# Group factors by a selection matmul, weights kept as stored pairs, the embedding product inside the gate's tile, norm chains put off, in the tail of a hybrid encoder layer

## The chip, the cores and the metric

The kernel runs on one core of one Trainium2 chip. The metric is the device time of one execution in microseconds (us); a lower one is better. Three runs of the kernel before took 1746.35, 1748.64 and 1754.81 us, so its median is 1748.64 us.

## The reference

One layer on x of 2048 tokens by 1024 features, all in float32:

```
h = RMSNorm(x);  cB, cC, ch, cz, q, k, v, az = split(h @ W_in)      # 8 x 512 columns
yc = cB * dwconv3_causal(cC * ch)                  # gated short convolution
ya = stick_breaking_attention(q, k, v)             # 8 heads x 64
y  = group_rmsnorm(concat(yc, ya), 64) * silu(concat(cz, az))       # 16 groups a token
x1 = x + y @ W_out
gate = sigmoid(RMSNorm(x1) @ W_pg + b)
x2 = x1 + gate * (p @ W_pe)                        # p: 256 features a token
out = RMSNorm(x2)
```

Stick-breaking attention takes, for a query t and keys s < t, the weight sigmoid(z_s) times the product of (1 - sigmoid(z)) over the keys between s and t. That running product is what the kernel computes as a scan along the keys.

## The kernel before, in words

**Layout.** Features lie on the 128 partitions, tokens along the free axis. The tokens are four chunks of 512, numbered 3, 2, 1, 0 in the order in which they are worked. A matrix product of full float32 quality is made of three passes: each operand is split into a rounded high part and a low part (`wh`, `wl` for a weight tile, `hh`, `hl` for an activation), and `product` (L230) issues high by high, high by low and low by high (L234, L235, L236), each 128 by 128 against 128 by 512. A tile of 128 output features takes 8 steps of contraction, so 24 matmuls.

**Weights.** `fetch_w` (L208) loads a raw half tile of weights (128 by 512, 256 KB) from DRAM, and `split_w` (L220) makes the pair of it: ScalarE copies the high part (L225), GpSimd subtracts for the low part (L226). That is done anew for each chunk in the tail: 16 tiles (8 of W_out, numbers 32 to 39, and 8 of W_pg, numbers 40 to 47) of two halves for each of four chunks, so 128 splits.

**Order of the program.** First come the projections of chunks 3 and 2 (`workE`), then those of chunks 1 and 0 (`workL`). Then the tail: for each chunk an `out_stage` (L630, product with W_out and x1) and a `gate_stage` (L685, product with W_pg, sigmoid, the embedding product with W_pe, x2). Every stage is a generator that yields after each step of contraction. `run` (L769) pulls 0.72 or 0.92 steps of the attention generator (L534) at each yield, so attention of all heads lies between the products, up to the end of chunk 1's `out_stage`; chunk 1's `gate_stage` must wait for chunk 0's attention, and from there on there is none. `later(n, f)` calls `f` n yields afterwards. Which order each engine's queue gets in the end is decided by a scheduler that keeps dependencies; each engine works its queue in order.

**Beside the stages.** `y_prep(c)` (L570) makes the W_out operand of chunk c: it multiplies y by the group factors and by the gate, and splits it. The factors lie with tokens on partitions (`rg`), so `expand` (L585) lets GpSimd copy each factor 64 or 16 times along the free axis, and four transposes (L604) bring that to features on partitions, five times a chunk, in the one PSUM bank `aux`. The norm of x1 is a chain: squares on ScalarE (L627), added up on GpSimd (L628), `norm_r` (L152: four matmuls by ones, L156, then a power on GpSimd, L161) and `norm_spread` (L166: four transposes, L171, and a copy). The factor `rB` of it is wanted first by the evacuation of the gate's first tile (L696). The norm of x2 is the same chain, started by `final` (L740).

**The embedding product.** In `gate_stage` each tile begins with six matmuls into a bank of its own (L722 to L724) with weights that `pe_weights` (L670) loads and splits for each chunk and tile (L679, L680). That bank is one of the two `mm` banks, which the gate's own tile (`pp`) also takes.

PSUM banks before: `z` 2, `mm` 2, `tr` 2 (attention's transposes), `av` 1, `aux` 1.

## Time and profile before

| | us |
|---|---|
| median of three runs | 1748.64 |
| the profiled execution | 1747.67 |
| its span, first to last instruction | 1745.9 |
| PE busy | 1614.3 (92%) |
| DVE busy | 1217.3 (70%) |
| POOL busy | 966.2 (55%) |
| ACT busy | 855.6 (49%) |
| mean DMA traffic | 141 GB/s |

PE is TensorE, DVE is VectorE, ACT is ScalarE, POOL is GpSimd, SP is the engine that issues most transfers. The busy share of PE is an average: it is 100% in some stretches and lower in the tail, and matmuls at a lower granted clock also count as busy. So the tail's stretches, their granted clock and what ended PE's idle time there are what to read.

### The profile page before, as it was taken

What the parts mean: (1) busy time and instruction counts of PE and PEld (TensorE: products, weight loads), DVE (VectorE), ACT (ScalarE), POOL (GpSimd) and SP (SyncE); (2) the same over time, 40 slices, a digit from 0 to 9 for tenths busy, and PEclk for the clock granted to TensorE, in tenths of its full rate; (3) what the DMA queues carried; (4) which work ended last, traced back from release to release, by engine and by line L of the source; (5) the groups of instructions that cost most, each with busy time, mean ns of one, the idle gap of its engine ahead of it and who ended that gap; (6) DMA issues with size and microseconds to landing.
All of it is one profiled execution on the core that took longest, in us unless ns stands there. A gap on an engine that the chain in (4) does not pass through costs nothing. (4 is left out here: it accounts for less than half of the span.)

```text
span 1745.9 us, 23060 instructions
## 1 busy us (share of the span) xinstructions
PE 1614.3 (92%) x7634; PEld 1309.7 (75%) x7634; DVE 1217.3 (70%) x1544; ACT 855.6 (49%) x1680; POOL 966.2 (55%) x891
## 2 busy tenths in 40 slices
...
GB/s 187 147 84 175 127 163 149 111 139 166 70 138 158 145 142 142 158 146 143 82 75 92 92 85 133 176 144 158 129 227 158 162 144 191 152 146 153 240 155 73
DMA packets 138632, 246.94 MB, mean 141 GB/s; under 512 B 16656, under 2 KB 20752, under 8 KB 138512
## 3 DMA queue, kind: packets, MB, share of 16 engines
...
HBM read 180.38 MB, written 65.01 MB: 141 GB/s over the span
## 5 line engine op out<-in xcount | busy, mean ns | idle before, releaser
L234 PE MATMUL pp<-hh,wh 128*128 128x512 f32 x1008 | 421.6, 418 | 2.1 <-ACT hh L138 2.1
L235 PE MATMUL pp<-hl,wh 128*128 128x512 f32 x1008 | 402.1, 399 | 1.2 <-DVE hl L141 1.2
L236 PE MATMUL pp<-hh,wl 128*128 128x512 f32 x1008 | 401.8, 399 | 0.0
L481 DVE TENSOR_TENSOR_SCAN T<-s,carry,small 128x513 f32<-128x513 f32 x192 | 293.5, 1529 | 98.0 <-ACT s L462 94.2
L462 ACT ACTIVATE s<-z 128x512 f32<-128x512 f32 (+1 forms) x320 | 171.5, 536 | 248.8 <-PE z L460 237.6
L487 POOL TENSOR_TENSOR b<-b,T 128x512 f32<-128x512 f32 (+2 forms) x160 | 179.7, 1123 | 150.2 <-DVE T L481 110.5
L226 POOL TENSOR_TENSOR wl<-wr,wh 128x512 fp32r<-128x512 f32 x126 | 176.3, 1401 | 101.3 <-ACT wh L225 95.3
L512 DVE TENSOR_TENSOR al<-tp,ah 128x512 fp32r<-128x512 f32 (+1 forms) x320 | 188.8, 597 | 59.2 <-ACT ah L509 58.1
L236 PEld LDWEIGHTS pp<-hh,wl 128*128 128x128 f32 x1008 | 192.1, 191 | 42.6
L234 PEld LDWEIGHTS pp<-hh,wh 128*128 128x128 f32 x1008 | 192.7, 191 | 32.9 <-ACT hh L138 2.4
L235 PEld LDWEIGHTS pp<-hl,wh 128*128 128x128 f32 x1008 | 193.3, 192 | 31.5 <-DVE hl L141 3.1
L509 ACT CAST ah<-tp 128x512 fp32r<-128x512 f32 (+1 forms) x320 | 166.1, 525 | 101.5 <-PE tp L504 99.9
L485 POOL COPY carry<-T 128x1 f32<-128x1 f32 x192 | 53.4, 278 | 277.6 <-DVE T L481 236.6
L504 PE MATMUL tp<-first,b 128*128 128x128 f32 x1088 | 177.0, 277 | 28.4 <-DVE al L512 25.0
L504 PEld LDWEIGHTS tp<-first,b 128*128 128x128 f32 x1088 | 138.8, 144 | 74.0 <-DVE al L512 33.2
L464 ACT ACTIVATE b<-z 128x512 f32<-128x512 f32 (+1 forms) x320 | 169.7, 530 | 0.0
L487 DVE TENSOR_TENSOR b<-b,T 128x512 f32<-128x512 f32 (+1 forms) x160 | 149.1, 932 | 10.4 <-DVE T L481 0.5
L479 DVE TENSOR_TENSOR_SCAN T<-s,first 128x129 f32<-128x129 f32 x128 | 84.0, 658 | 61.8 <-ACT s L462 58.1
L459 PE MATMUL z<-kk,q 128*128 128x512 f32 (+1 forms) x320 | 118.7, 371 | 5.9 <-DMA kk<-qk_d 3.9
L518 PE MATMUL av<-al,vv 128*128 128x512 f32 (+1 forms) x320 | 120.1, 376 | 1.8 <-DVE al L512 1.8
L517 PE MATMUL av<-ah,vv 128*128 128x512 f32 (+1 forms) x320 | 119.3, 373 | 0.0
L460 PE MATMUL z<-kk,q 128*128 128x512 f32 (+1 forms) x320 | 119.1, 372 | 0.0
...
## 6 DMA issues: line engine op xcount, KB each, us to landing
wr<-in_wst_dram SPq DMA_DIRECT2D x128, 256.0 KB, 2.7
vv<-v_d SPq DMA_DIRECT2D x80, 256.0 KB, 3.0
kk<-qk_d SPq DMA_DIRECT2D x80, 256.0 KB, 4.0
q<-qk_d SPq DMA_DIRECT2D x64, 256.0 KB, 3.7
...
v_d<-vo SPq DMA_DIRECT2D x32, 256.0 KB, 2.4
...
yt<-y_d SPq DMA_DIRECT2D x32, 256.0 KB, 2.9
```

Source lines behind the costliest of these rows:

```text
L226: nc.gpsimd.tensor_tensor(out=wl, in0=raw, in1=wh.bitcast(F32), op=ALU.subtract)
L234: nc.tensor.matmul(pp, wh[:, sl], hh, start=(kt == 0), stop=False)
L235: nc.tensor.matmul(pp, wh[:, sl], hl, start=False, stop=False)
L236: nc.tensor.matmul(pp, wl[:, sl], hh, start=False, stop=(kt == KT - 1))
L462: nc.scalar.activation(s[:, 1:w + 1], zp[:, 0:w], AF.Sigmoid, scale=-0.125)
L464: nc.scalar.activation(bt[:, 0:w], zp[:, 0:w], AF.Sigmoid, scale=0.125)
L481: nc.vector.tensor_tensor_scan(T[:, m:w + 1], s[:, m:w + 1], zeros.to_broadcast([P, w + 1 - m]), T[:, m - 1:m] if diag else carries[h, qc] ...
L487: eng.tensor_tensor(out=bt[:, 0:w], in0=bt[:, 0:w], in1=T[:, 0:w], op=ALU.mult)
L504: nc.tensor.transpose(tp[:, j * P:(j + 1) * P], bt[:, kb * P - k0:(kb + 1) * P - k0], ident)
L509: nc.scalar.copy(ah[:, 0:nj * P], tp[:, 0:nj * P])
L512: nc.vector.tensor_tensor(out=al[:, 0:w], in0=tp[:, 0:w], in1=ah[:, 0:w].bitcast(F32), op=ALU.subtract)
L518: nc.tensor.matmul(av[:, 0:w], v[:, kb], al[:, 0:w], start=False, stop=kc == 3 and kb == 0)
```

## The change

1. **Group factors.** `y_prep` no longer lets GpSimd copy factors. VectorE splits the 16 factors of a token into high and low parts (`r2`, 32 columns), four transposes turn them to 32 partitions (`rt`), and for each of the 8 feature tiles one matmul by a constant 0/1 matrix (`sel`, 32 rows, made once at the start on GpSimd) spreads them over the features.
2. **Stored pairs.** The pairs of W_out and W_pg are made once, in chunk 3, and stored to DRAM (`store_w`). For chunks 2, 1 and 0 `split_w` loads both parts straight into the buffers that the matmuls read. The pairs of W_pe are made once, beside two of chunk 1's and 0's projections (`pe_pairs`), stored, and loaded per tile (`pe_fetch`). One raw buffer fewer, one `w1` buffer more, one key buffer fewer.
3. **Embedding product.** Its six matmuls stand after the fourth step of the gate's tile (`embed`), in a `tr` bank.
4. **Norm chains put off.** `norm_r` and `norm_spread` for x1 stand 6 and 10 yields behind the `out_stage`; the evacuation of the gate's first tile is put off by 5; `final` begins 8 yields into the next `out_stage` and takes 4 yields a tile.
5. **Banks.** `aux` is gone and `tr` has three banks, shared by attention's transposes, group factors, norms, value transposes and the embedding product.
6. **Last chunk.** Sums of squares and x2 are added on VectorE, final_g is applied by ScalarE beforehand, and the last scaling reads the spread factor from PSUM, two tiles of eight on GpSimd, with stores from two queues.
7. The last two projection tiles run side by side (`proj_two`) with chunk 3's `y_prep`, at 0.5 attention steps per yield; four rows of attention (of 320) that stood ahead of chunk 3's `out_stage` now stand behind it, and the last three rows behind the start of chunk 1's `gate_stage`, where none stood. The store of x1 goes from ScalarE's queue to SP's.

On PE, at the passage from chunk 0's `out_stage` to its `gate_stage`, before (`pp40` is the gate's first tile, `ssp4` and `rT4` are the two PE steps of the norm of x1; ahead of these rows stand the six matmuls of the embedding product):

```order
L234 MATMUL pp40_('x1', 0)_16693<-hh_('x1', 0)_0_16294,wh('x1', 0)_40_0_16602 128x512
L235 MATMUL pp40_('x1', 0)_16693<-hl_('x1', 0)_0_16295,wh('x1', 0)_40_0_16602 128x512
L236 MATMUL pp40_('x1', 0)_16693<-hh_('x1', 0)_0_16294,wl('x1', 0)_40_0_16603 128x512
L234 MATMUL pp40_('x1', 0)_16693<-hh_('x1', 0)_1_16353,wh('x1', 0)_40_0_16602 128x512
L235 MATMUL pp40_('x1', 0)_16693<-hl_('x1', 0)_1_16354,wh('x1', 0)_40_0_16602 128x512
L236 MATMUL pp40_('x1', 0)_16693<-hh_('x1', 0)_1_16353,wl('x1', 0)_40_0_16603 128x512
L156 MATMUL ssp4_16661<-small_247,acc_('x1', 0)_16297 128x2 x4
L234 MATMUL pp40_('x1', 0)_16693<-hh_('x1', 0)_2_16401,wh('x1', 0)_40_0_16602 128x512
L235 MATMUL pp40_('x1', 0)_16693<-hl_('x1', 0)_2_16402,wh('x1', 0)_40_0_16602 128x512
L171 MATMUL rT4_16671<-first_241,rr_258 128x128 x4
```

The same place after the change (`px140` and `px141` are the gate's first and second tiles, `pe0_0` the embedding product):

```order
L788 MATMUL pe0_0_16602<-ph0_0_16532,we0_0_16582 128x512
L786 MATMUL pe0_0_16602<-ph0_1_16536,we0_0_16582 128x512
L787 MATMUL pe0_0_16602<-pl0_1_16537,we0_0_16582 128x512
L788 MATMUL pe0_0_16602<-ph0_1_16536,we0_0_16582 128x512
L179 MATMUL ssp4_16615<-small_319,acc0_16216 128x2 x4
L273 MATMUL px140_0_16584<-x1hh0_4_16429,wh40_241_16558 128x512
L274 MATMUL px140_0_16584<-x1hl0_4_16430,wh40_241_16558 128x512
```

And further on, to the passage to the gate's second tile:

```order
L273 MATMUL px140_0_16584<-x1hh0_7_16575,wh40_241_16558 128x512
L274 MATMUL px140_0_16584<-x1hl0_7_16576,wh40_241_16558 128x512
L275 MATMUL px140_0_16584<-x1hh0_7_16575,wl40_241_16559 128x512
L194 MATMUL rT4_16638<-first_313,rr_331 128x128 x4
L273 MATMUL px141_0_16645<-x1hh0_0_16212,wh41_242_16585 128x512
L274 MATMUL px141_0_16645<-x1hl0_0_16213,wh41_242_16585 128x512
```

The step by ones (L156, now L179) stood behind the embedding product and two steps of the gate's tile; now it stands behind four steps and the embedding product. The transposes (L171, now L194) stood two matmuls further on; now they stand behind the whole first tile.

On SP in chunk 0's `out_stage`, before (`wr` a raw half of weights, `of` a tile of chunk 1's x2, `xr` a tile of x, `out_0` the output):

```order
L214 DMA wr('y', 0)_36_1_16368<-in_wst_dram 128x512
L133 DMA of1_6_16302<-o_d1_6_221 128x512
L759 DMA out_0_dram<-of1_3_16274 128x512
L759 DMA out_0_dram<-of1_4_16281 128x512
L759 DMA out_0_dram<-of1_5_16288 128x512
L133 DMA xr0_2_16305<-in_xt_dram 128x512
L133 DMA of1_7_16319<-o_d1_7_222 128x512
L759 DMA out_0_dram<-of1_6_16302 128x512
L133 DMA xr0_3_16361<-in_xt_dram 128x512
L214 DMA wr('y', 0)_37_0_16386<-in_wst_dram 128x512
```

And after the change (`wh` and `wl` the parts of a half tile, `wp` their place in DRAM, `x1_d` the store of x1):

```order
L256 DMA wh36_232_16335<-wp_d36_0_0_255 128x512
L256 DMA wl36_232_16336<-wp_d36_0_1_256 128x512
L708 DMA x1_d0_2_177<-xr0_2_16218 128x512
L156 DMA of1_4_16347<-o_d1_4_219 128x512
L853 DMA out_0_dram<-of1_2_16295 128x512
L256 DMA wh36_233_16356<-wp_d36_1_0_257 128x512
L256 DMA wl36_233_16357<-wp_d36_1_1_258 128x512
L156 DMA of1_5_16367<-o_d1_5_220 128x512
L853 DMA out_0_dram<-of1_3_16315 128x512
L156 DMA xr0_5_16384<-in_xt_dram 128x512
L256 DMA wh37_234_16387<-wp_d37_0_0_259 128x512
L256 DMA wl37_234_16388<-wp_d37_0_1_260 128x512
```

Each half of weights is two loads where it was one, and the stores of x1 stand in the same queue. From the first load of the W_out weights of chunk 0 to the first of its W_pg weights SP has 46 transfers before and 68 after the change (11.9 and 17.8 MB); in chunk 3's `gate_stage` 61 and 103 (15.1 and 27.0 MB). From the first load for chunk 3's `out_stage` to the end of chunk 0's, SP moves 94.7 MB before and 143.1 MB after.

The core of the diff:

```diff
-        RAWS = 3
+        RAWS = 2
...
+        def paired(t, tag):
+            return t >= OUT0 and tag[1] < 3
...
         def split_w(pool=pj, tags=("wh", "wl")):
 
-            if raws:
-                t, tag, f, raw = raws.pop(0)
-                wh, wl = [pool.tile([P, CH], F32R, tag=x, bufs=4, name=f"{x}{tag}_{t}_{f}") for x in tags]
-                nc.scalar.copy(wh, raw)
-                nc.gpsimd.tensor_tensor(out=wl, in0=raw, in1=wh.bitcast(F32), op=ALU.subtract)
-                wt[t, tag, f] = (wh, wl)
+            n = made[0]
+            if n < 2 * len(wq):
+                (t, tag), f = wq[n // 2], n % 2
+                made[0] += 1
+                wh, wl = wt[t, tag, f] = [
+                    pool.tile([P, CH], F32R, tag=x, bufs=4, name=f"{x}{t}_{n}") for x in tags]
+                if paired(t, tag):
+                    for w, d in zip((wh, wl), wp_d[t, f]):
+                        nc.sync.dma_start(w.bitcast(F32), d)
+                else:
+                    raw = raws.pop(0)
+                    nc.scalar.copy(wh, raw)
+                    nc.gpsimd.tensor_tensor(out=wl, in0=raw, in1=wh.bitcast(F32), op=ALU.subtract)
+                    if t >= OUT0:
+                        later(3, store_w, t, f, wh, wl)
             fetch_w()
+
+        def store_w(t, f, *pair):
+            for w, d in zip(pair, wp_d[t, f]):
+                nc.sync.dma_start(d, w.bitcast(F32))
...
+                    pp = bank("mm", 2, f"pp{t}_{c}")
+                    for kt in range(KT):
+                        if (i, n, kt) in ((0, 0, 0), (0, 0, 4), (1, 0, 4), (1, 1, 0)):
+                            split_w()
+                        product(pp, t, tag, c, kt)
+                        if kt == KT - 1:
+                            evacs[n](c, pp)
+                        if i:
+                            next(besides, None)
+                        yield
+            for _ in besides:
+                yield
...
                 if besides is not None:
                     next(besides, None)
                 yield
+                if kt == 3 and between is not None:
+                    yield from between()
...
+            fetch(0)
+            r2 = pj.tile([P, 4, 32], F32R, tag="r2", bufs=1, name=f"r2_{c}")
+            rs = rg[:, 4 * c:4 * c + 4]
+            nc.vector.tensor_copy(r2[:, :, 0:16], rs)
+            nc.vector.tensor_tensor(out=r2[:, :, 16:32], in0=rs, in1=r2[:, :, 0:16].bitcast(F32),
+                                    op=ALU.subtract)
+            yield
+            yield
+            turned = bank("tr", 3, f"rt{c}")
+            for b in range(4):
+                nc.tensor.transpose(turned[0:32, b * P:(b + 1) * P], r2[:, b].bitcast(F32), ident)
+            rt = buf("u", f"rs{c}", F32R, CH + 2)
+            nc.scalar.copy(rt[0:32, 0:CH], turned[0:32])
+            yield
+            yield
+            for kt in range(KT):
+                fetch(kt + 1)
+                gT = bank("tr", 3, f"gT{c}_{kt}")
+                j = max(kt - 3, 0) * P
+                nc.tensor.matmul(gT, sel[0:32, j:j + P], rt[0:32, 0:CH], start=True, stop=True)
...
+        def norm_of(slot, key):
+            assert counts[key] == KT
+            norm_r(slot, accs[key])
...
-                    squares(("x1", c), m, x1)
-                    nc.scalar.dma_start(x1_d[c][m], x1)
+                    later(1, squares, ("x1", c), m, x1, nc.vector if c == 0 else nc.gpsimd)
+                    later(2, lambda: nc.sync.dma_start(x1_d[c][m], x1))
...
-
-            def spread():
-                norm_r(slot, accs["x1", c])
-                later(3, norm_spread, slot)
-            later(2, spread)
-
-        ph, pw = {}, {}
-
-        def p_prep(c):
+            later(6, norm_of, slot, ("x1", c))
+            later(10, norm_spread, slot)
+
...
-        def pe_weights(c, m):
-            if m == KT:
-                return
-            raw = buf("w1", f"we{c}_{m}")[:, 0:2 * P]
...
-            later(3, split)
+        def pe_pairs():
+
+            for m in range(KT):
+                raw = buf("w1", f"we{m}")[:, 0:2 * P]
+                nc.sync.dma_start(raw, wpe_d[m])
+                yield
+                yield
+                t = buf("sl", f"wes{m}", F32R)
+                nc.scalar.copy(t[:, 0:2 * P], raw)
+                nc.gpsimd.tensor_tensor(out=t[:, 2 * P:4 * P], in0=raw, in1=t[:, 0:2 * P].bitcast(F32),
+                                        op=ALU.subtract)
+                yield
+                yield
+                nc.sync.dma_start(we_d[m], t.bitcast(F32))
+
+        pw = {}
+
+        def pe_fetch(c, m):
+            if m < KT:
+                pw[c, m] = buf("sg", f"we{c}_{m}", F32R)
+                nc.sync.dma_start(pw[c, m].bitcast(F32), we_d[m])
 
...
+            def embed(m):
+
+                def f():
+                    w = pw.pop((c, m))
+                    pe = bank("tr", 3, f"pe{c}_{m}")
+                    for kt in range(2):
+                        h, l = ph[c, kt]
+                        hi, lo = [w[:, (2 * i + kt) * P:(2 * i + kt + 1) * P] for i in range(2)]
+                        nc.tensor.matmul(pe, hi, h, start=(kt == 0), stop=False)
+                        nc.tensor.matmul(pe, hi, l, start=False, stop=False)
+                        nc.tensor.matmul(pe, lo, h, start=False, stop=(kt == 1))
+                        if kt == 0:
+                            yield
+                    es[m] = buf("sh", f"e{c}_{m}")
+                    nc.scalar.copy(es[m], pe)
+                    pe_fetch(c, m + 1)
+                    xs[m] = load(x1_d[c][m], f"x1r{c}_{m}")
+                    yield
+                return f
...
+            def evac(m):
+                def f(pp):
+                    later(5 if m == 0 else 0, sigmoid, m, pp)
+                return f
+
+            def sigmoid(m, pp):
+                g = buf("gg", f"g{c}_{m}")
+                nc.vector.tensor_tensor(out=g, in0=pp, in1=rB[slot], op=ALU.mult)
+                nc.scalar.activation(g, g, AF.Sigmoid, bias=b_pg[:, m:m + 1])
+                later(2, mix, m, g)
+
+            def mix(m, g):
+                x1 = xs.pop(m)
+                nc.vector.tensor_tensor(out=g, in0=g, in1=es.pop(m), op=ALU.mult)
+                o = resident[m] if c == 0 else g
+                adds.tensor_tensor(out=o, in0=x1, in1=g, op=ALU.add)
+                later(2 if c else 0, total, m, o)
+
+            def total(m, o):
+                squares(("o", c), m, o, adds)
+                if c:
+                    later(1, lambda: nc.sync.dma_start(o_d[c][m], o))
+                else:
+                    nc.scalar.activation(o, o, AF.Copy, scale=g_fin[:, m:m + 1])
+
+            pe_fetch(c, 0)
+            side = twice() if besides is not None else None
+            for m in range(KT):
+                yield from stage(GATE0 + m, ("x1", c), evac(m), side, embed(m))
+            if besides is not None:
+                for _ in besides:
+                    yield
+
...
+        def final(c):
+
+            for _ in range(8):
+                yield
+            norm_of(8 + c, ("o", c))
+            for _ in range(5):
+                yield
+            norm_spread(8 + c)
...
+                for _ in range(4):
                     yield
...
+                later(2, lambda o=o, m=m: nc.sync.dma_start(out_d[c, m], o))
+
+        def final_last():
+
+            norm_of(8, ("o", 0))
+            r = rr[:, 64:68]
+            rT = bank("tr", 3, "rT8")
+            for b in range(4):
+                nc.tensor.transpose(rT[:, b * P:(b + 1) * P], r[:, b:b + 1].to_broadcast([P, P]), ident)
+            spread = buf("rB", "rB8")
+            nc.scalar.copy(spread, rT)
+            for m in range(KT):
+                o = resident[m]
+                on_pool = m in (1, 4)
+                eng = nc.gpsimd if on_pool else nc.vector
+                eng.tensor_tensor(out=o, in0=o, in1=spread if on_pool else rT, op=ALU.mult)
+                (nc.scalar if m % 2 else nc.sync).dma_start(out_d[0, m], o)
...
@@ -800,6 +910,8 @@
                     b = besides
                     if chunks == cE and (kind, i) in (("g", 1), ("g", 2)):
                         b = (norm_later(cL[i - 1]),) * 2
+                    if chunks == cL and (kind, i) in (("g", 0), ("g", 1)):
+                        b = (pairs_e,) * 2
                     add(work, gate, t, gi, chunks, b, tiles=[(t, chunks[0])])
...
-        workL = pairs_of(cL, orderL, last=y_prep(3), first_besides=ahead(splits(0), 2))
+        pairs_e = pe_pairs()
+        workL = pairs_of(cL, orderL[:-2], first_besides=ahead(splits(0), 2))
+
+        work2 = []
+        add(work2, lambda: proj_two((3, 15), cL, (evac_b(3), evac_gate(15, 3)), ahead(y_prep(3), 2)),
+            tiles=[(3, cL[0]), (15, cL[0])])
...
             def gates(c=c):
-                p_prep(c)
-                pe_weights(c, 0)
-                tick_all()
                 return gate_stage(c, y_prep(c - 1) if c else None)
             add(tail[-1], gates, need=[(h, c - 1) for h in range(NH)] if c else [],
                 tiles=[(GATE0 + m, ("x1", c)) for m in range(KT)])
         run(workL, RATE_L)
+        run(work2, RATE_Y)
```

## Rows read from the trace of the kernel before

**Rows 1.** Busy time by stretch: us, PE, PEld, DVE, ACT, POOL, PEclk, DMA share, GB/s
```profile
950.00:1050.00 100.00, 100.00 (x493) 82.27 (x492) 86.02 (x103) 50.89 (x98) 53.70 (x53) 1.00 0.26 81
1056.50:1536.10 479.60, 417.47 (x1945) 332.76 (x1944) 385.73 (x417) 269.01 (x520) 345.44 (x307) 0.94 0.52 162
1536.10:1612.70 76.60, 65.11 (x279) 52.21 (x278) 26.43 (x34) 32.13 (x57) 52.16 (x44) 0.89 0.50 154
1612.70:1665.40 52.70, 49.42 (x212) 39.03 (x210) 25.47 (x28) 22.05 (x38) 34.10 (x26) 0.97 0.70 231
1665.40:1726.80 61.40, 58.00 (x246) 46.99 (x246) 12.90 (x16) 25.11 (x44) 44.55 (x37) 0.94 0.34 103
1726.80:1745.90 19.10, 2.98 (x12) 2.50 (x12) 6.94 (x11) 1.94 (x3) 3.54 (x3) 0.60 0.30 110
1640.00:1650.00 10.00, 9.75 (x42) 7.22 (x40) 4.48 (x6) 4.26 (x7) 5.60 (x5) 1.00 0.91 308
```
**Rows 2.** PE's waits from 1056.5 us on: waiter, releaser, us in total, times, longest
```profile
PE tp L504 <- DVE al L512: 15.3, 11, 3.0
PE pe L722 <- ACT wes L679: 12.0, 3, 7.6
PE gT L604 <- DVE yt L606: 10.1, 7, 3.7
PE ssp L156 <- POOL acc_('o', 0)_16764 L628: 5.7, 1, 5.7
PE gT L604 <- POOL rb L590: 5.6, 2, 4.8
PE ssp L156 <- POOL acc_('o', 3)_11974 L628: 5.0, 1, 5.0
PE rT L171 <- POOL rr L161: 4.9, 8, 1.4
...
PE pp_('x1', 1)_15777 L234 <- DVE g L696: 3.0, 1, 3.0
...
PE ssp L156 <- POOL acc_('x1', 1)_14862 L628: 0.8, 1, 0.8
...
PE pp_('x1', 0)_16693 L234 <- DVE xr L641: 0.3, 1, 0.3
```
**Rows 3.** PE in order of time about one stall: start, us, what, idle before
```profile
1569.63 0.79 PE L722 MATMUL pe<-ph,wes 128*128 128x512 f32 x1 [7.55 <-ACT wes L679]
...
1572.56 0.63 PE L234 MATMUL pp_('x1', 1)_15850<-hh_('x1', 1)_0_14859,wh('x1', 1)_42_0_15778 128*128 128x512 f32 x1
1572.98 0.63 PE L235 MATMUL pp_('x1', 1)_15850<-hl_('x1', 1)_0_14860,wh('x1', 1)_42_0_15778 128*128 128x512 f32 x1
...
1573.71 0.40 PE L234 MATMUL pp_('x1', 1)_15850<-hh_('x1', 1)_1_14969,wh('x1', 1)_42_0_15778 128*128 128x512 f32 x1
1573.94 0.40 PE L235 MATMUL pp_('x1', 1)_15850<-hl_('x1', 1)_1_14970,wh('x1', 1)_42_0_15778 128*128 128x512 f32 x1
```
**Rows 4.** POOL's busy time of the weights' low parts in the tail (L226)
```profile
1056.50:1726.80 670.30, 180.71 (x125) 0.94 0.51 161
```
**Rows 5.** DVE in order of time: the same operation twice
```profile
1497.35 0.75 DVE L141 SCALAR_TENSOR_TENSOR hl_('x1', 1)_3_15166<-xr,cst,hh_('x1', 1)_3_15165 128x512 fp32r<-128x512 f32 x1 [0.60 <-ACT hh_('x1', 1)_3_15165 L138]
1514.89 1.89 DVE L141 SCALAR_TENSOR_TENSOR hl_('x1', 1)_5_15351<-xr,cst,hh_('x1', 1)_5_15350 128x512 fp32r<-128x512 f32 x1 [0.20 <-ACT hh_('x1', 1)_5_15350 L138]
```
**Rows 6.** Transfers: what, count, KB each, us from issue to landing
```profile
wr<-in_wst_dram SPq DMA_DIRECT2D x128, 256.0 KB, 2.7
...
wr('y', 0)_37_0_16386<-in_wst_dram SPq DMA_DIRECT2D x1, 256.0 KB, 6.0
```
**Rows 7.** All engines in order of time, the end
```profile
1726.83 0.69 DVE L696 TENSOR_TENSOR g<-pp_('x1', 0)_17106,rB 128x512 f32<-128x512 f32 x1 [4.66 <-PE pp_('x1', 0)_17106 L236]
...
1729.08 1.26 POOL L705 TENSOR_TENSOR o<-x1r,g 128x512 f32<-128x512 f32 x1 [3.50 <-DVE g L703]
1730.38 0.63 ACT L627 ACTIVATE sq_('o', 0)_7_17139<-o 128x512 f32<-128x512 f32 x1 [2.10 <-POOL o L705]
1731.08 1.26 POOL L628 TENSOR_TENSOR acc_('o', 0)_16764<-acc_('o', 0)_16764,sq_('o', 0)_7_17139 128x512 f32<-128x512 f32 x1 [0.74 <-ACT sq_('o', 0)_7_17139 L627]
...
1736.77 0.59 ACT L173 COPY rB<-rT 128x512 f32<-128x512 f32 x1 [5.76 <-PE rT L171]
1737.39 5.39 DVE L757 SCALAR_TENSOR_TENSOR o<-o,cst,rB 128x512 f32<-128x512 f32 x8 [2.92 <-ACT rB L173]
```

209 lines of the change are left out of this document (94 added, 115 removed).

## The prediction

> **What bounds the kernel now.** I read the busy time by stretch first, then PE's waits, then single stretches in order of time. From 950 to 1050 us PE is busy all the time at full clock: 493 matmuls in 100 us, 0.203 us each, wide and narrow ones mixed as attention and products mix them [rows 1]. So nothing but PE's own work bounds the kernel there, and DVE at 86% keeps up. The tail is different. Chunks 3, 2 and 1 up to the end of chunk 1's out_stage (1056.5 to 1536.1 us) have 1945 matmuls; at 0.203 us that is 395 us, and they take 479.6: 85 us are lost. In the three stages behind it nearly all matmuls are wide; two of them start 0.23 us apart at full clock [rows 3]. Chunk 1's gate_stage is 279 times 0.23, 64 us, and takes 76.6; chunk 0's out_stage 212, 49 us, and takes 52.7; its gate_stage 246, 57 us, and takes 61.4. With the 12, 4 and 5 us of these, 106 us of the tail are not PE's work, and 19.1 us more follow the last product [rows 1].
>
> Two things make up the 106 us. PE waits by name for what the change touches [rows 2]: the embedding weights' split (12.0 us), the group factors (10.1 and 5.6), the sums of the norms (seven rows from 5.0 to 0.8, the one at the very end left out: 17.7), the norm's power (4.9, of which 1.4 at the end: 3.5), and a bank still being evacuated (six rows from 3.0 to 0.3: 7.9). That is 56.7 us. Beside them stand 15.3 us of attention's transposes waiting for VectorE. The second is the clock. Behind the 7.55 us stall at 1569.63 two products start 0.42 us apart instead of 0.23 [rows 3]: PE runs at the lower of its two levels, 1.2 GHz, for a while after a stall. A granted clock of 0.94 over 479.6 us is 58 us at half speed, 0.89 over 76.6 is 17, 0.97 over 52.7 is 3, 0.94 over 61.4 is 7: 85 us in all [rows 1]. Half of that, less the fifth in which PE waits anyway, is 34 us lost.
>
> **The change part by part.**
> *Waits.* The norm of x1 is the test case. The rows of the end show what the chain takes from the last product to the ones: from 1726.83 to behind the last sum at 1732.34, 5.5 us [rows 7]; for x1 it is a step shorter. Ahead of the ones PE now has four steps of the gate's tile and the embedding product, 18 matmuls or 4.1 us, where it had two steps, and between ones and transposes the other half tile, 12 matmuls or 2.8 us. In chunks 3 to 1 attention's matmuls come on top. So the wait is covered or nearly so. The embedding weights come from DRAM a tile ahead, without ScalarE or GpSimd. The embedding product leaves the two banks of the gate's tiles, so a tile no longer waits for the evacuation of the one before it. The group factors need one matmul each, with nothing on GpSimd ahead. Of the 56.7 us I take back 85%: 48. What is late next is attention's transposes behind VectorE, which the change leaves.
>
> *Clock.* The waits named are 57 of about 80 us of waits in the tail, so 0.7 of the 34 us: 24, of which I take 22.
>
> *GpSimd's work.* 96 of the 128 low parts of weights go. They cost 180.71 us for the 125 in the trace, 1.45 each [rows 4]: 139 us less on GpSimd, which is busy 345 of 479.6 us in the first stretch. GpSimd bounds nothing by itself there. But the same VectorE operation took 0.75 us in one place and 1.89 in another [rows 5], so VectorE is held up by something. The Trainium skill ("SBUF — State Buffer", Who interferes with whom) says that a VectorE instruction with two inputs in SBUF and a GpSimd instruction that reads SBUF block each other; the rows fit it, and by that rule each removed split gives VectorE back up to its own length. Without it I have only that 1.14 us of difference and the 15.3 us of waits for VectorE: the gain lies between 0 and 15, and I take 5, as chunk 3 still splits.
>
> *Group factors on PE.* 80 narrow transposes go; 16 narrow transposes and 32 wide matmuls of 32 rows come. No row shows such a matmul; taken as wide ones the 48 are 11 us, and the 80 that go are at most 18 by the same price. I take 0, with +5 to -7 as bounds. The eight small operations on VectorE are less than 0.69 us each (the nearest, a whole 512-wide one [rows 7]): under 6 us, hidden where VectorE is not last.
>
> *The end.* Two GpSimd additions of 1.26 become VectorE's at 0.69, the 0.59 us copy leaves the path, and 6 instead of 8 scalings follow [rows 7] (5.39 us for 8, so 1.3 less): -3.
>
> *Transfers.* This is what the change pays with. Chunk 0's out_stage issues 17.8 MB instead of 11.9, beside chunk 1's final. The fastest 10 us of that stage moved 308 GB/s with the DMA engines 0.91 busy [rows 1]; at that rate 17.8 MB are 58 us, while PE needs 49 and the stage takes 52.7 now. The Trainium skill ("DMA: Bandwidth & Descriptors", Specifications) gives about 358 GB/s as the limit of HBM for one core; by that the stage could be done in 50 us (an estimate), and the transfers would cost nothing there. No run here has shown that rate over a stage, so I go by the row: +5, bounds 0 and +9. From chunk 3's out_stage to chunk 0's the tail moves 143 MB instead of 95; in the 549 us that I expect for it (608.9 less 60) that is 260 GB/s, with 231 the highest of a whole stage so far [rows 1]. For loads that come late I add 4, bounds 0 and +40.
>
> *Attention's end.* Fewer steps are pulled beside chunk 3's y_prep, so four rows of keys are worked later, and the last ones alone with the first tile of chunk 1's gate: +4, bounds 0 and +8.
>
> *Start.* GpSimd builds the selection matrix among the first splits: eight instructions of the kind and size of those whose longest row is 1.26 us, 0 to 10 us, mostly while it waits for weights: +1.
>
> Sum: -48 -22 -5 -3 +5 +4 +4 +1 = -64. The profiled execution took 1747.67 us, so 1684; it lay 1 us under the median of three, so 1685 against that median.
>
> **The rivals.** *PE as dense as from 950 to 1050.* Then the stretches are 395, 64, 55, 57 and 16 us behind 1056.5: 1643.5, with 1.8 around the span and 1 for the median 1646. For it: there PE lost nothing beside VectorE at 86%. Against: the tail has more of VectorE's work for the same PE time, 385.7 us against 395.
> *VectorE sets the pace.* It is busy 385.7 of 479.6 us [rows 1]. If it gets no shorter and never passes 86%, the stretch takes 448: 31 us gained, then 10 in chunk 1's gate_stage, 4 in chunk 0's, 3 at the end, and 10 of costs: 1710. For it: the longest wait of rows 2 is of that kind.
> *Transfers set the pace.* If the tail's 143 MB go at 245 GB/s, halfway from 231 to 260, they take 584 us against 608.9: 25 gained, 4 and 3 behind, 1 lost at the start: 1718. For it: a load of weights took 6.0 us to land in chunk 0's out_stage against 2.7 in the middle of all [rows 6].
> *Slower: loads come too late for the tile.* A pair is loaded one tile ahead, 24 matmuls or 5.5 us where no attention lies between, in SP's queue in order, behind stores that wait for VectorE or GpSimd; before, the raw half had been fetched further ahead. With 6 us to land PE would stand at each of the 96 half tiles of chunks 2 to 0. The point from which it decides is 0.67 us a half tile (64 us over 96); at 1 us, and some clock lost with it, it is 1684 + 96 + 5 = 1785. Against it: attention doubles the lead for chunks 2 and 1.
> *The waits only move.* The norm's chain stays as long, and PE meets it 4 us later: then the 21 us of norms and their clock stay, 1685 + 29 = 1714; it is in the cases above as their upper part.
>
> **How the numbers follow.** Forecast 1685 (1662 to 1705) 0.48; PE dense 0.15; VectorE 0.15; transfers 0.15; too late 0.07. About 0.5% (8.7 us) can be told from no change: faster by more is the first four less the slow edge of the transfers, 0.89; the same 0.04; slower 0.07. The range of 1645 to 1726 leaves the slower case and a part of the transfers' outside.
>
> **What would show it.** In the profile after: no wait of PE for the embedding weights, and the norms' ones together under 5 us; granted clock 0.97 or more from 1056 us on; GpSimd's busy time lower by about 150 us; VectorE's scans and products shorter in chunks 2 and 1; chunk 0's out_stage 55 to 58 us with over 300 GB/s. It is wrong if PE waits for wh or wl by name, if attention's transposes wait for VectorE for over 30 us, or if the stretches before 1020 us have changed by more than 10 us.

## The result and the profile after

The changed kernel takes 1681.29 us (median of four runs, 1678.39 to 1681.41). Its time is 0.9606 of the time of the kernel before, 95% interval 0.9579 to 0.9632: faster, by about 67 us. The forecast was 1685. The profiled execution took 1681.41 us, with a span of 1679.7.

The stretches of [rows 1], found anew by the same products (chunks 3 to 1 up to the end of chunk 1's out_stage; chunk 1's gate_stage; chunk 0's out_stage; its gate_stage; the end), in the columns of that group:

```profile
1051.60:1474.00 422.40, 396.87 (x1878) 316.97 (x1877) 346.68 (x408) 229.01 (x444) 229.51 (x219) 0.97 0.78 260
1474.00:1552.70 78.70, 75.21 (x342) 57.12 (x341) 41.19 (x55) 31.96 (x56) 31.31 (x24) 1.00 0.65 209
1552.70:1605.70 53.00, 48.69 (x205) 37.67 (x204) 21.94 (x33) 11.79 (x19) 4.04 (x3) 0.97 0.96 327
1605.70:1662.00 56.30, 56.30 (x253) 46.06 (x251) 20.89 (x31) 20.37 (x32) 1.01 (x1) 1.00 0.61 199
1662.00:1679.70 17.70, 2.80 (x13) 2.24 (x12) 6.61 (x11) 2.66 (x4) 3.51 (x3) 0.63 0.32 119
```

Against [rows 1] they changed by -57.2, +2.1, +0.3, -5.1 and -1.4 us, and the tail starts 4.9 us sooner. The whole tail in one row, of before:

```profile
1056.60:1745.90 689.30, 592.88 (x2689) 473.43 (x2687) 457.36 (x506) 350.18 (x659) 479.69 (x415) 0.93 0.51 159
```

and of after:

```profile
1051.60:1679.70 628.10, 579.87 (x2685) 460.06 (x2683) 437.31 (x537) 295.79 (x554) 269.38 (x250) 0.97 0.75 250
```

The two rows divide the tail's 61.2 us: PE idles 48.2 us instead of 96.4, and is busy 13.0 us less, at a granted clock of 0.97 instead of 0.93. The number of matmuls is nearly the same, but not the work. The tail of after holds four rows of attention more (part 7 of the change), 32 matmuls, as the number of attention's transposes shows, before and after:

```profile
L504 PE MATMUL tp<-first,b 128*128 128x128 f32 x364 | 60.0, 283 | 15.6 <-DVE al L512 15.3
L569 PE MATMUL tp<-first,b 128*128 128x128 f32 x380 | 60.5, 280 | 14.6 <-DVE al L577 9.7 <-DVE yt L667 4.3 <-ACT e L792 0.6
```

Four rows are 16 wide matmuls, 0.23 us apart [rows 3], and 16 transposes, of which four take 0.35 us (1033.21 to 1033.56 us of the kernel before): about 5 us, an estimate. Without them PE would be busy some 18 us less. For the group factors 24 wide matmuls and 12 transposes stand in the tail in place of 72 transposes, by these prices about the same time. PE's waits in the tail (columns as in [rows 2]):

```profile
PE tp L569 <- DVE al L577: 9.7, 4, 4.7
PE gs L425 <- ACT sq L418: 5.0, 2, 3.2
PE ssp L179 <- DVE acc L688: 4.4, 1, 4.4
PE tp L569 <- DVE yt L667: 4.3, 2, 2.4
PE py L273 <- DMA wh<-wp_d: 4.2, 3, 1.9
PE av L583 <- DVE al L577: 4.1, 6, 1.1
...
PE rT L194 <- POOL rr L184: 1.5, 1, 1.5
...
PE ssp L179 <- POOL acc L688: 0.4, 1, 0.4
```

Of the waits of [rows 2], those for the embedding weights, the group factors and a tile's bank have no row any more (the turned factors are waited for once, 1.1 us); the norms' ones wait 0.4 us (the 4.4 belong to the very end); attention's transposes wait 9.7 us for `al` instead of 15.3, but 4.3 us for `yt`, that is, for one of the three shared banks, in which VectorE still reads the group factors. New is the wait for `wh` from DRAM: 4.2 us, all of it in chunk 0's out_stage. Transfers in the page of after, as in [rows 6]:

```profile
wh<-wp_d SPq DMA_DIRECT2D x96, 256.0 KB, 4.0
wl<-wp_d SPq DMA_DIRECT2D x96, 256.0 KB, 4.3
```

Ahead of the tail the net gain of 4.9 us hides two movements. Two stretches of before, the first projections from their 192nd product on, and the first convolution tiles of the second ones:

```profile
87.70:519.60 431.90, 419.41 (x2055) 346.20 (x2054) 291.66 (x433) 193.63 (x404) 194.93 (x175) 0.99 0.43 131
790.10:858.00 67.90, 66.97 (x334) 55.03 (x334) 51.13 (x68) 34.86 (x68) 27.30 (x34) 1.00 0.36 115
```

and the same products of after:

```profile
89.80:512.80 423.00, 414.98 (x2055) 342.40 (x2054) 298.76 (x436) 194.19 (x407) 196.66 (x175) 1.00 0.44 134
781.30:854.40 73.10, 69.21 (x335) 56.32 (x334) 51.76 (x68) 36.77 (x76) 35.73 (x42) 0.98 0.49 153
```

The first won 8.9 us; the second, in which the embedding's pairs are made (eight GpSimd instructions more), lost 5.2. The last stretch ahead of the tail, which the four rows of attention left and to which most of chunk 3's `y_prep` came, took 132.6 us instead of 134.1. The first 192 products lost 2.9, where a row of after shows chunk 2's first parts waiting for a bank that VectorE reads (start, us, what, idle before):

```profile
36.91 0.76 PE L273 MATMUL pp<-hhh,wh 128*128 128x512 f32 x1 [6.42 <-DVE vT L350]
```

### The profile page after: what moved, and what is told of

It reads as the page before. It is cut to its first block, busy times and chain, and to the rows that moved or that the text cites. A ratio compares the mean times of both kernels' runs of the same rounds, so it can differ in the third digit from the quotient of the medians.

```text
span 1679.7 us, 22914 instructions
## 1 busy us (share of the span) xinstructions
PE 1594.1 (95%) x7602; PEld 1285.6 (77%) x7602; DVE 1192.5 (71%) x1572; ACT 797.9 (48%) x1572; POOL 767.6 (46%) x739
## 4 chain that ended last, share of the span: by engine, by line
PE 34%; DVE 5%; POOL 3%; issue 3%; DMA 3%; ACT 2%; SPq 0%; DVEq 0%; POOLq 0%; ACTq 0%
PE px L273 3%; PE pp L273 3%; PE pp L275 3%; PE pp L274 3%; PE px L274 3%; PE px L275 3%; PE tp L569 3%; DVE T L546 2%; PE py L273 2%; PE py L274 2%; PE py L275 2%; PE av L583 2%; PE z L525 1%; PE av L582 1%; PE z L524 1%
## 5 line engine op out<-in xcount | busy, mean ns | idle before, releaser
L273 PE MATMUL pp<-hhh,wh 128*128 128x512 f32 x1008 | 419.8, 416 | 8.4 <-DVE vT L350 6.4
L274 PE MATMUL pp<-hhl,wh 128*128 128x512 f32 x1008 | 400.3, 397 | 4.0 <-DVE hhl L164 3.9
L275 PE MATMUL pp<-hhh,wl 128*128 128x512 f32 x1008 | 398.9, 396 | 0.0
L260 POOL TENSOR_TENSOR wl<-wr,wh 128x512 fp32r<-128x512 f32 x158 | 224.3, 1421 | 108.9 <-ACT wh L259 98.8
L275 PEld LDWEIGHTS pp<-hhh,wl 128*128 128x128 f32 x1008 | 190.9, 189 | 42.3
L577 DVE TENSOR_TENSOR al<-tp,ah 128x512 fp32r<-128x512 f32 (+1 forms) x320 | 188.0, 597 | 49.4 <-ACT ah L574 47.9
L273 PEld LDWEIGHTS pp<-hhh,wh 128*128 128x128 f32 x1008 | 191.3, 190 | 39.7 <-issue 7.8
L274 PEld LDWEIGHTS pp<-hhl,wh 128*128 128x128 f32 x1008 | 192.0, 191 | 34.6 <-DVE hhl L164 6.8
L552 DVE TENSOR_TENSOR b<-b,T 128x512 f32<-128x512 f32 (+1 forms) x160 | 137.2, 858 | 11.0 <-DVE T L546 0.9
L259 ACT CAST wh<-wr 128x512 fp32r<-128x512 f32 x158 | 98.6, 625 | 84.4 <-PE pp L274 56.1
L524 PE MATMUL z<-kk,q 128*128 128x512 f32 (+1 forms) x320 | 118.8, 371 | 4.3 <-DMA kk<-qk_d 2.3
```

Of the source, the lines that this page charges most:

```text
L260: nc.gpsimd.tensor_tensor(out=wl, in0=raw, in1=wh.bitcast(F32), op=ALU.subtract)
L273: nc.tensor.matmul(pp, wh[:, sl], hh, start=(kt == 0), stop=False)
L274: nc.tensor.matmul(pp, wh[:, sl], hl, start=False, stop=False)
L275: nc.tensor.matmul(pp, wl[:, sl], hh, start=False, stop=(kt == KT - 1))
L552: eng.tensor_tensor(out=bt[:, 0:w], in0=bt[:, 0:w], in1=T[:, 0:w], op=ALU.mult)
L577: nc.vector.tensor_tensor(out=al[:, 0:w], in0=tp[:, 0:w], in1=ah[:, 0:w].bitcast(F32), op=ALU.subtract)
```

## The experiments

Ratios are to the kernel before, run on the same chip, with 95% intervals; the changed kernel's is 0.9606 (0.9579 to 0.9632). Differences in us are of medians, against 1681.3. On the chips of these runs the medians of the kernel before lay between 1746.1 and 1748.9 us, so a difference under 3 us tells nothing.

| kernel | median us | ratio (interval) | against after |
|---|---|---|---|
| a_split_again: pairs undone | 1709.1 | 0.9787 (0.9770 to 0.9805) | +28 |
| a_banks_apart: turned-about banks undone | 1706.4 | 0.9777 (0.9757 to 0.9797) | +25 |
| a_norms_early: norm chains not put off | 1694.9 | 0.9702 (0.9676 to 0.9728) | +14 |
| a_factors_old: group factors as before | 1681.2 | 0.9621 (0.9606 to 0.9637) | 0 |
| b_pairs: before with pairs alone | 1729.5 | 0.9884 (0.9868 to 0.9900) | |
| c_act_busy: idle ScalarE copies | 1682.0 | 0.9628 (0.9611 to 0.9646) | +1 |
| c_pool_busy: idle GpSimd subtractions | 1777.7 | 1.0174 (1.0154 to 1.0194) | +96 |
| a_out0_split | 1687.3 | 0.9646 (0.9626 to 0.9665) | +6 |
| a_start_z | 1680.4 | 0.9615 (0.9600 to 0.9629) | -1 |
| a_rate_y | 1679.0 | 0.9599 (0.9584 to 0.9614) | -2 |
| c_all_pairs | 1692.2 | 0.9690 (0.9669 to 0.9711) | +11 |
| c_best | 1677.0 | 0.9595 (0.9576 to 0.9614) | -4 |

**The pairs undone.**

```diff
-            return t >= OUT0 and tag[1] < 3
+            return False
...
-                    if t >= OUT0:
-                        later(3, store_w, t, f, wh, wl)
```

> The changed kernel, with one of its parts undone: every weight of W_out and W_pg is split on the chip anew in each chunk, by ScalarE and GpSimd, and no pair is stored or loaded. The theory (the gain is TensorE's waits and the clock that they lowered) puts the relief of GpSimd at 5 us and takes the embedding weights' wait (12 us before) to come back in part, against 16.9 MB fewer stores and loads: 1690 us, anywhere in 1677 to 1698, with out0 down from 53 to 49 or 50 us since its loads are single again. Rival (GpSimd's 180 us of splits, by way of VectorE's slower operations beside them, were the main cost): 1715 us or more, with VectorE's scans back at 1.53 us from 1.48.

+28, between the two and nearer to the rival. The tail of this kernel, and the two longest of PE's waits in it:

```profile
1051.50:1705.50 654.00, 590.45 (x2685) 466.77 (x2683) 472.62 (x537) 347.47 (x649) 418.19 (x345) 0.95 0.55 176
```
```profile
PE tp L567 <- DVE al L575: 16.0, 5, 4.7
PE av L581 <- DVE al L575: 8.4, 7, 2.0
```

With the same 537 instructions VectorE is busy 35.3 us longer than after (472.6 against 437.3), beside 148.8 us more of GpSimd. PE idles 15.3 us more than after and is busy 10.6 us longer; it waits 24.4 us for `al`, where after it waits 13.8. No weight is waited for. Which instructions grow is seen in VectorE's groups of the tail: `al` has one operand in PSUM, `b` both in SBUF (count, then busy us and mean ns). Before:

```profile
L512 DVE TENSOR_TENSOR al<-tp,ah 128x512 fp32r<-128x512 f32 (+2 forms) x101 | 62.2, 628 | 9.8 <-ACT ah L509 9.7
L487 DVE TENSOR_TENSOR b<-b,T 128x512 f32<-128x512 f32 (+1 forms) x47 | 51.3, 1091 | 2.9
```

After:

```profile
L577 DVE TENSOR_TENSOR al<-tp,ah 128x512 fp32r<-128x512 f32 (+1 forms) x104 | 63.9, 629 | 6.4 <-ACT ah L574 5.9
L552 DVE TENSOR_TENSOR b<-b,T 128x512 f32<-128x512 f32 (+1 forms) x49 | 45.1, 921 | 3.9 <-DVE T L546 0.5
```

With the pairs undone:

```profile
L575 DVE TENSOR_TENSOR al<-tp,ah 128x512 fp32r<-128x512 f32 (+1 forms) x104 | 63.9, 629 | 6.6 <-ACT ah L572 6.3
L550 DVE TENSOR_TENSOR b<-b,T 128x512 f32<-128x512 f32 (+1 forms) x49 | 54.5, 1113 | 3.5
```

`al` stays at 628 to 629 ns in all three; `b` goes from 1091 to 921 and back to 1113.

By stage, between the same products, the run also shows what the pairs cost. Chunk 3's out_stage, without its stores, is 5.1 us shorter than after, and chunk 0's out_stage, whose loads are single again, takes 47.9 us instead of 53.0 (the expectation had 49 or 50):

```profile
1578.50:1626.40 47.90, 46.83 (x206) 38.40 (x206) 26.89 (x33) 21.17 (x36) 26.11 (x20) 0.96 0.82 268
```

The four stages of chunks 2 and 1 are 29.3 us longer together. By the rows of the two tails (GB/s times us) the edit takes 42 MB from the tail, not the 16.9 of the expectation.

**The pairs alone, put into the kernel before.**

```diff
+                if paired(t, tag):
+                    for wx, d in zip((wh, wl), wp_d[t, f]):
+                        nc.sync.dma_start(wx.bitcast(F32), d)
+                else:
...
+                    if t >= OUT0:
+                        later(3, store_w, t, f, wh, wl)
```

> The kernel before, with one part of the change alone: W_out's and W_pg's split weights are stored once and loaded as pairs in the three later chunks; all else as before. Theory (the gain lies in TensorE's waits, of which only the embedding weights' 12 us hang on GpSimd's queue): 1749 - 10 to 15 = 1734 to 1739 us. Rival 1 (GpSimd's relief, with VectorE and its evictions quicker, is the main gain): 1749 - 35 = 1714 us or less. Rival 2 (the loads come late, twice the bytes in the tail): over 1749 us.

-19, between the theory and the first rival. Its tail, VectorE's `b` in it, and PE's waits:

```profile
1053.10:1727.80 674.70, 586.49 (x2689) 471.50 (x2687) 416.10 (x506) 297.15 (x563) 335.94 (x319) 0.93 0.68 223
```
```profile
L507 DVE TENSOR_TENSOR b<-b,T 128x512 f32<-128x512 f32 (+1 forms) x47 | 39.1, 831 | 3.2 <-ACT b L484 0.6
```
```profile
PE gT L624 <- DVE yt L626: 10.4, 6, 3.7
PE pe L742 <- ACT wes L699: 9.7, 2, 7.9
PE pp_('y', 0)_16389 L256 <- DMA wl('y', 0)_35_0_16347<-wp_d: 6.8, 1, 6.8
...
PE gT L624 <- POOL rb L610: 5.7, 3, 4.8
```

The waits for the embedding weights (12.0 before) and the group factors (10.1 and 5.6) [rows 2] stay nearly whole: they didn't hang on the weights' splits in GpSimd's queue. With the same 506 instructions VectorE is busy 41.3 us less than before, beside 143.8 us less of GpSimd; `b` falls from 1091 to 831 ns. The granted clock of the tail stays at 0.93. The second rival holds in one place: PE waits 6.8 us for a half tile of chunk 0's W_out, and chunk 0's out_stage takes 9.0 us more than before, between the same products.

**The same instructions with nothing behind them,** on GpSimd and on ScalarE.

```diff
                 if paired(t, tag):
...
+                    idler = pj.tile([P, CH], F32, tag="wr", bufs=RAWS, name=f"idler{n}")
+                    nc.gpsimd.tensor_tensor(out=idler, in0=sel[:, 0:CH].bitcast(F32),
+                                            in1=sel[:, P:P + CH].bitcast(F32), op=ALU.subtract)
```

> The changed kernel with one thing added: for each of the 96 half tiles whose pair is loaded, GpSimd subtracts two tiles of constants into a buffer that nobody reads, an instruction of the shape and size of the split that the pair saves. No weight waits for it, ScalarE does nothing more, no byte is moved more or less. Undoing the pairs cost 28 us. Theory (GpSimd's work beside VectorE's is what costs: with it VectorE's operation on two SBUF tiles took 1113 ns instead of 921, and PE waited longer for attention's probabilities): +15 to +28 us, 1696 to 1709, the same lengthening of VectorE's operations with two SBUF inputs, none of those that read PSUM. Rival (weights made on the chip come late, or ScalarE's copies hold up attention): under +5 us.

```diff
+                    nc.scalar.copy(idler, sel[:, 0:CH].bitcast(F32))
```

> The changed kernel with one thing added: for each of the 96 half tiles whose pair is loaded, ScalarE copies a tile of constants into a buffer that nobody reads, of the shape and size of the copy that the pair saves. Theory (the 28 us of the pairs are GpSimd's): within 5 us of 1681. Rival (ScalarE's queue, in which attention's exponentials and copies stand, is what the pairs relieve): +10 us or more, VectorE's operations unchanged in length.

The first went otherwise than both said, and is no clean measurement: with nothing to wait for, the 96 subtractions were not spread over the half tiles but stand in GpSimd's order close together, from 1207 to 1367 us. GpSimd there (in order of time), and PE behind it:

```profile
1297.72 2.48 POOL L258 TENSOR_TENSOR idler<-sel 128x512 f32<-128x512 f32 x2
1300.17 1.25 POOL L691 TENSOR_TENSOR acc<-acc,sq 128x512 f32<-128x512 f32 x1
```
```profile
1301.48 0.80 PE L179 MATMUL ssp<-small,acc 128*128 128x2 f32 x3 [23.04 <-POOL acc L691]
```

Work that PE needs stood behind idle work in an engine that serves in order; that is where the 96 us went: the products before 1207 us come when they do after, those behind 1367 us come 97 us later. One number of it still serves: over its tail VectorE is busy 470.0 us with 537 instructions, 32.7 more than after, beside 132.7 us more of GpSimd. Here and with the pairs undone VectorE loses 0.25 and 0.24 us for each us of GpSimd; with the pairs put into the kernel before it won 0.29. The Trainium skill ("SBUF — State Buffer", Who interferes with whom) says that a VectorE instruction with two SBUF inputs and a GpSimd instruction that reads SBUF exclude each other, and one with a single SBUF input does not; the rows of `b` and `al` agree. The 96 copies on ScalarE (46 us more of it, also close together) cost nothing that can be measured: as far as copies in one block can show it, ScalarE is not what the pairs relieve.

**Norm chains not put off.**

```diff
-            later(6, norm_of, slot, ("x1", c))
-            later(10, norm_spread, slot)
+            later(2, norm_of, slot, ("x1", c))
+            later(5, norm_spread, slot)
```

> The changed kernel, with the norm chains as early as they were: power two steps and ones product five steps after a stage's end, and the final part's start not put off. The theory has the seven norm products wait about 17 us again, beside 3.5 us for the power, and a colder clock behind each: 1681 + 20 = 1701 us (1695 to 1710), the waits by name being for VectorE's accumulators and for the norm's power. Rival (the waits only move: what is not waited for here is waited for a few products later): within 4 us of 1681.

(The first tile's evacuation and the start of the final part are put back likewise.) +14. Its tail, and its longest wait; the profiled execution is the slowest of the five, 7 us above their median:

```profile
1059.10:1700.20 641.10, 589.59 (x2685) 467.43 (x2683) 430.90 (x537) 297.29 (x554) 266.66 (x250) 0.95 0.73 245
```
```profile
PE ssp L179 <- POOL acc L688: 12.5, 6, 3.8
```

The norms wait 12.5 us instead of 0.4, but in this execution's tail PE idles only 3.3 us more than after (other waits shrink), and is busy 9.7 us longer at a clock of 0.95 instead of 0.97. The rival is half right, on the waits. How the 14 us of the median divide is not shown: PE's order is that of after up to 1135 us, yet this execution is 7.5 us late where the tail begins, and over its whole length the clock was 0.967, in the other four 0.974 to 0.976, in those of after 0.977 to 0.979.

**Group factors as before.**

```diff
-                nc.tensor.matmul(gT, sel[0:32, j:j + P], rt[0:32, 0:CH], start=True, stop=True)
+                for b in range(4):
+                    nc.tensor.transpose(gT[:, b * P:(b + 1) * P], rb[:, b * P:(b + 1) * P], ident)
+                if 3 <= kt < KT - 1:
+                    rb = expand(kt + 1)
```

> The changed kernel, with the group factors spread as before, by GpSimd copies and four transposes for a feature tile in place of one selection product. The theory: 15.7 us of TensorE's waits for these copies come back in part, with the clock behind them and 48 more narrow transposes: 1681 + 15 to 25 = 1696 to 1706 us. Rival (with the pairs stored GpSimd is free, and its copies are in time without the selection product): within 5 us of 1681, with no wait for the copies by name.

The rival holds in its time: no difference. A wait of 6.6 us for the copies is there all the same, and is made up for:

```profile
PE gT L665 <- POOL rb L651: 6.6, 2, 4.6
```

The 10.1 us of `gT` behind `yt` don't come back: they were a wait for the bank, which VectorE was still reading. With the pairs alone, and one bank, they had stayed (10.4).

**The turned-about banks as before:** transposes two, all else one; but the embedding product, which stood in `mm` before, is in that one bank too.

```diff
-                    tp = bank("tr", 3, f"tp{n}_{kb}")
+                    tp = bank("tr", 2, f"tp{n}_{kb}")
...
-                gT = bank("tr", 3, f"gT{c}_{kt}")
+                gT = bank("aux", 1, f"gT{c}_{kt}")
...
-                    pe = bank("tr", 3, f"pe{c}_{m}")
+                    pe = bank("aux", 1, f"pe{c}_{m}")
```

> The changed kernel with its three turned-about PSUM banks as they were, two for the transposes and one for norms, embedding products and first parts. The stretch before 1020 us, which no part of the change was costed in, is 3.6 us shorter at its end and 8.8 us shorter at its best point. Theory: the third bank gives this, by transposes that waited 2.8 to 3.2 us for attention's probabilities at 242, 265 and 327 us; here the 8 us come back, and in the tail the embedding product waits for its only bank: 1689 to 1695 us. Rival (the 3.6 us are spread from run to run, or come from the order alone): within 3 us of 1681 before 1020 us.

+25, more than the theory had; the profiled execution is the slowest of the four, 6 us above their median. PE's waits in its tail, and its first projections:

```profile
PE pe L786 <- DVE yt L667: 11.6, 5, 4.0
...
PE gT L665 <- ACT e L792: 3.5, 2, 2.3
PE gT L665 <- DVE yt L667: 3.1, 3, 2.5
```
```profile
93.70:527.10 433.40, 419.75 (x2053) 346.22 (x2052) 295.52 (x435) 195.00 (x407) 194.67 (x174) 0.99 0.43 130
```

Group factors and embedding products wait 18 us in one bank, 15 of them for each other's evacuation. The kernel before had no such pairing, so the tail's share of the 25 us is not what a third bank is worth against it. From the 192nd product on the first projections take 433.4 us, as before (431.9) and with the pairs alone (430.1), where after took 423.0; seven other kernels here that keep the three banks and add nothing to that stretch took 422.2 to 424.4. The third bank gives these 9 to 10 us. Of the rest of the 20.7 us by which the tail starts later, 3.9 lie ahead of that stretch and 6.5 in the stages behind it.

**Smaller ones.** Chunk 0's W_out split on the chip; other banks at the start; attention's rate in the last two projection tiles:

```diff
-            return t >= OUT0 and tag[1] < 3
+            return t >= OUT0 and tag[1] < 3 and not (t < GATE0 and tag[1] == 0)
```

> The changed kernel, but chunk 0's W_out weights are loaded once and split on the chip, as before, instead of being loaded as pairs: out0 (the stage with 17.8 MB in 53.0 us) moves 4 MB less. Theory (this stage is bound by its transfers, which the three waits of 4.2 us for the stored halves show): out0 53 to 49 us, no wait for a stored half in it, 1677 us. Rival (the splits put back on ScalarE and GpSimd cost VectorE what the transfers gave): 1680 to 1684 us.

The edit missed its aim: a tile that is split is also stored, so that chunk 0's out_stage moved 345 GB/s over 58.3 us, 20.1 MB, against 327 over 53.0, 17.3 MB. It shows the reverse of what was meant: 2.8 MB more, and 5.3 us more. That fits the theory, but doesn't test it alone, as PE waits 6.5 us there for halves that are split on the chip (ScalarE in its turn 9.5 us for the raw ones from DRAM). That the bytes set this stage's length is seen better with the pairs undone: with 12.8 MB it takes 47.9 us, and PE is busy for 46.8 of them.

```profile
1553.30:1611.60 58.30, 48.36 (x206) 37.64 (x204) 27.05 (x34) 20.05 (x34) 22.21 (x17) 0.97 0.99 345
```

```diff
-                pp = bank("mm", 2, f"pp{t}_{c}") if c == 3 else bank("tr", 3, f"pp{t}_{c}")
+                pp = bank("mm", 2, f"pp{t}_{c}") if c == 3 else bank("z", 2, f"pp{t}_{c}")
```

> The changed kernel, with the parts of chunk 2 that are computed at the start in banks of the attention's sums instead of the turned-about ones. Theory: the new wait of 6.4 us at 36.9 us for VectorE's eviction goes, and all later work comes 4 to 6 us sooner: 1676 us. Rival (the end of the first stage is set by its loads, so that the wait is taken later): 1681 us.

The rival: no difference. The 6.42 us are gone, and PE waits 4.21 us, 6 us later, for the squares of chunk 2's norm:

```profile
42.49 1.65 PE L179 MATMUL ssp<-small,xsq 128*128 128x2 f32 x7 [4.21 <-DVE xsq L210]
```

The shared bank isn't what costs at the start: with the banks of before (a_banks_apart) the first 192 products take 86.4 us, against 82.7 after and 79.8 before. What does stays open.

```diff
-RATE_E, RATE_L, RATE_Y = 0.72, 0.92, 0.5
+RATE_E, RATE_L, RATE_Y = 0.72, 0.92, 0.92
```

> The changed kernel, but with attention's last chunks taken beside out0 and gate0 at the rate 0.92 instead of 0.5, as the rest has it. The prediction put the end of attention, which now lies in gate1, at +4 us. Theory: gate1 (78.6 us against 76.6 before, the only stage of the tail that grew) is long because attention's last steps follow one another there; at another rate some of it is spread over the products of out0 and gate0: 1677 to 1681 us. Rival (it takes the place of the products that hide out0's transfers): 1681 to 1686 us.

Chunk 1's gate_stage falls from 78.6 to 72.0 us, but the last projection tiles take 5 us longer; 2 us are left, too few to tell.

**Pairs made ahead,** for all four chunks:

```diff
+                    raw = load(wst_d[t, f], f"wa{t}_{f}")
...
+                    nc.scalar.copy(high, raw)
+                    nc.gpsimd.tensor_tensor(out=raw.bitcast(F32R), in0=raw, in1=high.bitcast(F32), op=ALU.subtract)
...
+                    for w, d in zip((high.bitcast(F32), raw), wp_d[t, f]):
+                        nc.sync.dma_start(d, w)
```

> The changed kernel with the pairs of W_out and W_pg made ahead: during the first projections (90 to 510 us), where TensorE had 8 us of idle time in 423 and GpSimd is busy 46%, all 32 halves are loaded, split and stored, and chunk 3's two stages load pairs as the others do. Theory (each GpSimd split costs where VectorE is what TensorE waits for: 28 us for 96 in the tail, nothing where TensorE is dense): 32 fewer splits in chunk 3's stages, -9 us there, 0 to +4 in the first projections: 1672 to 1676 us. Rival (chunk 3's stages have attention in plenty and no wait for it): 1681 to 1686 us.

> The changed kernel with two things that the other runs point to: the pairs of W_out and W_pg made ahead, but spread thinly, one half tile for every 26 steps over the whole of the first and second projections (in the run that made one in 9 steps, chunk 3's stages won 16 us and the first projections lost 21), and attention's rate 0.92 in the last two projection tiles (2 us). Theory (the loss there came of bunching: stores that wait on SP's queue for GpSimd and ScalarE hold up the loads behind them): 16 and 2 us gained, 0 to 8 lost: 1663 to 1671 us. Rival (each half tile costs its 0.66 us wherever it is made before the tail): 1681 to 1686 us.

Neither run came out as its theory or its rival had it: 1692 and 1677 us. Chunk 3's two stages won in both, and the first projections paid. Both stretches after:

```profile
7.10:512.80 505.70, 481.40 (x2325) 391.49 (x2326) 353.06 (x506) 229.49 (x478) 235.21 (x210) 0.98 0.45 138
1051.60:1233.40 181.80, 164.73 (x767) 130.78 (x766) 148.23 (x168) 103.39 (x202) 129.75 (x110) 0.95 0.80 265
```

with a half tile every 9 steps:

```profile
6.60:535.00 528.40, 488.92 (x2325) 394.56 (x2326) 366.27 (x506) 244.24 (x510) 283.72 (x242) 0.97 0.57 180
1075.30:1240.90 165.60, 159.74 (x768) 126.68 (x767) 131.17 (x166) 87.65 (x172) 77.89 (x79) 0.99 0.72 238
```

and with one every 26 (where attention's rate moved work too):

```profile
7.00:518.00 511.00, 483.92 (x2326) 392.62 (x2327) 363.30 (x507) 237.47 (x496) 263.46 (x227) 0.98 0.52 163
1063.20:1234.60 171.40, 163.00 (x773) 129.83 (x771) 133.27 (x170) 88.91 (x172) 80.97 (x83) 0.97 0.71 230
```

The price in the first projections falls from 23 to 5 us when the work is thinned out. By GpSimd's count 32 half tiles are made there in the dense version and 17 in the thin one, so a half tile costs 0.7 and 0.3 us: not a fixed price. What it consists of stays open: from 85 to 400 us of the dense version PE's waits name ScalarE, VectorE and late keys, a few us each, and no one of them explains 23. The longest:

```profile
PE gs L435 <- ACT sq L428: 6.1, 3, 2.9
```

That stores on SP's queue hold up the loads behind them, as the expectation had it, was argued and is not shown. The thin version comes to 1677.0 us, the lowest median of all, but its interval overlaps the changed kernel's: better than before, not shown to be better than the change.

## Why the prediction came out right, and where its steps were wrong

The sum held: -64 forecast, -66 in the profiled executions. That waits of PE and the clock behind them make up the tail is borne out: idle time fell by 48.2 us, where the term for waits had -48, or -43 with the terms for GpSimd, the end, the transfers and attention's end. The clock's term of -22 is too large: 13.0 us less of busy time, or some 18 with the four rows of attention taken out, for which the sum had +4. The 4.9 us ahead of the tail had not been costed. That the sum comes so close is in part luck: 9 us too much on busy time stand against 5 too little on idle time and 6 ahead of the tail, where +1 was put.

Of the signs named, the waits for embedding weights and norms, VectorE's shorter scans (1529 ns instead of 1610) and GpSimd's time (199 us less) came as said. The clock was 0.97 or more in the stretches of [rows 1] up to the end, but 0.95 in chunk 3's two stages by themselves. Chunk 0's out_stage was shorter than the 55 to 58 us named.

The steps that say which edit brings it were wrong in three places:

- *GpSimd's work, -5, bounds 0 and -15.* Undoing the pairs costs 28 us, putting them in alone brings 19. The step took 1.14 us of difference between two rows as worth little, since GpSimd bounds nothing by itself; but 35 us of VectorE's time hang on it, VectorE's part of attention's probabilities (`al`) is what PE then waits for (24.4 us against 13.8), and the clock is lower too (0.95 against 0.97). That VectorE's time hangs on GpSimd's is shown in three runs; that the 28 us come by this route alone is argued from these rows, as the run that was to show it put its work in one block. The rule that was set beside the rows spoke for more than was taken.
- *Waits, the share of the group factors.* 10.1 of their 15.7 us were put down to GpSimd's copies and four transposes; they were a bank's. The selection product, the edit named first, brings nothing that can be measured beside the other edits.
- *The third bank,* counted only where a gate's tile waited for its bank (7.9 us). Undoing it costs 25 us, most of it ahead of the tail, where nothing had been forecast beyond +1 for the start. There it won 9 us, which the stretch in which the pairs of the embedding weights are made (+5.2) and the start (+2.9) mostly gave back; what costs in these two was not tested.

The norm chains are as forecast in size (17.7 and 3.5 us of waits with their share of the clock; 14 measured), though how these divide into waits and clock is not shown. Undoings of 28, 25, 14 and 0 add up to the whole, but they needn't: the pairs are worth 19 without the rest and 28 with it.

The transfers were costed from a row of 308 GB/s, which gave 58 us for chunk 0's out_stage and +5; it took 53.0, at 327. The +5 was the right size all the same: with the pairs undone the stage takes 47.9, and the other edits win there what the transfers cost (52.7 before). The Trainium skill ("DMA: Bandwidth & Descriptors", Specifications) has about 358 GB/s for a core's share of HBM, by which it would have been 50 (an estimate). That figure did not bind this kernel, which has one core running: 14 us of chunk 0's out_stage went at 380 GB/s, and 30 us of a_out0_split, from that stage into the next, at 363:

```profile
1586.00:1616.00 30.00, 21.60 (x75) 15.35 (x74) 13.99 (x16) 7.57 (x13) 6.64 (x5) 0.89 1.01 363
```

The prediction called it a sign against itself if PE waited for `wh` by name; it does, for 4.2 us, the +4 that late loads were given. With attention's end in it (342 matmuls instead of 279) chunk 1's gate_stage grew by 2.1 us, where +4 was put. The end brought 1.4 instead of 3.

Of the rivals, VectorE's had the condition that it gets no shorter, and it did: 346.7 us instead of 385.7, 82% of 422.4. With the pairs undone it is at 83% of that stretch (368.9 of 442.2 us), and the 1709 us are near that rival's 1710; that they come by its mechanism is not shown. The late loads stayed at 4.2 us; PE as dense as in [rows 1] was not reached, with 48.2 us of idle time left in the tail.

## What to carry to other kernels

An engine that bounds nothing can still be what a change pays for: price its work by what it does to the instructions beside it, and compare the mean of the same instruction with and without that neighbour. A wait named for an evacuation can be a wait for the bank, as it was here; count banks before crediting it to the producer. And test the edits of a bundle one by one even when the sum fits: here the sum was right to 4 us, and the edit named first brought nothing.

## What the runs showed of the chip beyond that

- VectorE lost 0.24 to 0.29 us for each us that GpSimd worked beside it, whether that work was spread or close together; its instruction with an operand in PSUM stayed at 628 to 630 ns.
- Either of the two can be the one that takes longer. In [rows 5] GpSimd splits a weight beside both instructions: its split takes 1.82 us beside the one of 0.75 us (from 1497.43 us) and 1.29 us beside the one of 1.89 us (from 1514.94 us).
- A stage of transfers ran at 345 GB/s for 58 us with the DMA engines 0.99 busy (a_out0_split), 30 us of it and the next at 363.
- The price of the lower clock was small for its length: a granted clock of 0.93 over the tail's 689.3 us is 97 us at half speed, 0.97 over 628.1 is 38; PE was busy 13.0 us less with four rows of attention more, some 18 us less without them (an estimate): 0.2 to 0.3 us for each of those 59.
